# Queries doubled by transfers within SBUF, fox scores in two matmuls

## The chip, the cores and the metric

The kernel runs on one core of a Trainium2 chip, as one program. The metric is the device time of that core in microseconds (us), median of several executions. The engines are TensorE (PE in the profile), VectorE (DVE), ScalarE (ACT), GpSimd (POOL) and SyncE (SP, which here issues transfers only).

## The reference

Two transformer blocks follow each other on 512 positions of width 1024, in fp32. The first (latent attention beside a state-space scan, about 345 us) is not touched. The second has two layers, each with an attention mixer and an MLP of width 4096. The mixer has 8 "nsa" heads, each with a compressed, a selected and a window branch, and 8 "fox" heads, all of 64 dimensions. A fox head is causal attention in which running sums of log forget gates are added to the scores:

```python
log_f = jax.nn.log_sigmoid(f_logits.astype(jnp.float32) + f_bias.astype(jnp.float32))
cum = jnp.cumsum(log_f, axis=1).transpose(0, 2, 1)
for i in range(s // Q_BLOCK):
    q0, q1 = i * Q_BLOCK, (i + 1) * Q_BLOCK
    logits = (jnp.einsum('bhqd,bhkd->bhqk', q[:, :, q0:q1], k[:, :, :q1]).astype(jnp.float32) * scale
              + cum[:, :, q0:q1, None] - cum[:, :, None, :q1])
    mask = jnp.arange(q1)[None, :] <= jnp.arange(q0, q1)[:, None]
    p = _masked_softmax(logits, mask)
    outs.append(jnp.einsum('bhqk,bhkd->bhqd', p.astype(v.dtype), v[:, :, :q1]))
```

The term of the query, `cum[..., q0:q1, None]`, is the same along a row and falls out of the softmax; only that of the key is computed. With 512 positions all eight blocks of 64 keys are selected for every query, so that the selected and the window branch of an nsa head are each causal attention over all 512 keys, with rotated queries and keys of their own.

## The kernel before

TensorE gets fp32 accuracy from fp32r operands by splitting a number into a high part `hi` and the rest `lo`. A projection takes three matmuls a tile (hi by hi, hi by lo, lo by hi; lines 174 to 176). For scores the 64 dimensions leave half of the 128 contraction rows free, and the kernel fills them. `stacked` puts the keys' hi into one half and their lo into the other, for both heads of a pair (tiles `ka`, `kb`). `doubled` puts the queries' hi into both halves (`qh1`, `qh2`), and their lo into both halves (`ql1`, `ql2`). Then a score tile is two matmuls: the queries' hi over hi and lo of the keys (line 911), and the queries' lo over the same (line 914). A fox head has a third between them (line 913): a one-hot weight, `ohr`, picks the head's running sums out of `cumr`, which holds hi and lo of the sums of all heads on rows of their own. `attend` runs this for four blocks of 128 queries, over 512, 384, 256 and 128 keys, each followed by a VectorE instruction that adds the mask and takes the row's extreme (line 915), ScalarE's exponential (918), POOL's scaling (927), transposes on TensorE (940), a split of the transposed weights by ScalarE and VectorE (`pt`, lines 143 and 144) and the products with the values (949, 950).

`doubled` starts from a projected pair of heads: head 1 in partitions 0 to 63, head 2 in 64 to 127. ScalarE copies the hi part of all (871) and two halves into the other place (873, 875), VectorE copies the hi half that stays (874), POOL subtracts for lo in one instruction of 128 partitions (`lo`, 864), and VectorE copies three halves of it (876 to 878). It runs 8 times a layer: for four pairs of nsa queries, behind the rope, and for four pairs of fox queries.

The rope swaps rows of a pair by four small transfers that ScalarE's queue issues into a `swap` tile (1065); VectorE multiplies it (1066), POOL multiplies the source (1067), VectorE adds (1068). There are NSW = 2 such tiles, used in turn, first by the two tiles of nsa keys (`kf`) and then by the query pairs.

The order of the heads is n0 f0 n1 f1 n2 f2 n3 f3 (pairs). The 12 projections of query and key pairs run as fillers between the steps of the heads, so that a pair is projected shortly before it is attended; their weights are loaded one job ahead or more. The order of instructions on each engine is fixed when the program is built, by a scheduler that simulates a timeline; tiles come from pools with a given number of slots (`S`, `Q`, `PT`, `K`), and a tile that reuses a slot waits for the slot's last reader. SP issues all weight loads in its order.

Of the kernel before, what the change touches and what calls it, by code (L numbers as in the profile page):

```python
# [9 lines left out]
F32 = mybir.dt.float32  # L10
# [17 lines left out]
SL0 = 3  # L28
NSW = 2
UP = (3,)  # L30
# [6 lines left out]
BANKS2 = {"g": (0, 6), "sc": (0, 3), "o": (3, 5), "mm": (5, 6), "tr": (6, 8)}  # L37
SLOTS2 = {"S": 12, "PT": 6, "K": 4, "Q": 8, "c": 2, "ch": 1, "tb": 3, "e8": 2, "w": 4}

# [24 lines left out]
class Net:  # L64
# [782 lines left out]
    def setup2(self):  # L847
        c = lambda n, sh: self.const(n, sh, pool=self.spool)
        nc = self.nc
        self.mask = c("mask", [128, 512])  # L850

        self.swaps = [self.spool.tile([128, 512], F32, name=f"swap{i}") for i in range(NSW)]
        for t in self.swaps:
            nc.gpsimd.memset(t, 0.0)
        self.swap = itertools.cycle(self.swaps)
        self.cmask = c("cmask", [128, 4, 31])
        cv = c("cvalid", [128, 5])
        self.cvalid, self.sgn = cv[:, 0:4], cv[:, 4:5]
        oh = c("onehot", [128, 8])
        self.oh = self.spool.tile([128, 8], F32R, name="ohr")  # L860
        nc.vector.tensor_copy(self.oh, oh)

    def lo(self, out, src, hi):
        self.nc.gpsimd.tensor_tensor(out, src, hi.bitcast(F32), OP.subtract)

    def doubled(self, src, tag):

        nc = self.nc
        h1, h2, l1, l2 = (self.act(F32R, name=n, tag=tag) for n in ("qh1", "qh2", "ql1", "ql2"))
        lw, up = slice(0, 64), slice(64, 128)  # L870
        nc.scalar.copy(h1, src)
        self.lo(l1, src, h1)
        nc.scalar.copy(h2[lw], src[up])
        nc.vector.tensor_copy(h2[up], h1[up].bitcast(F32))
        nc.scalar.copy(h1[up], src[lw])
        nc.vector.tensor_copy(l2[up], l1[up].bitcast(F32))
        nc.vector.tensor_copy(l2[lw], l1[up].bitcast(F32))
        nc.vector.tensor_copy(l1[up], l1[lw].bitcast(F32))
        return (h1, l1), (h2, l2)

    def stacked(self, src, tag):
# [9 lines left out]

    def attend(self, q, k, rgate, v, o, first, last, cum=None):

# [9 lines left out]
        for group in ((3,), (2,), (0, 1)):  # L903
            bank = self.ps("sc")
            c = 0
            for i in group:
# [3 lines left out]
                c += w  # L910
                mm(p, q[0][:, qs], k[:, :w], start=True, stop=False)  # L911
                if cum is not None:
                    mm(p, cum[0], cum[1][:, :w], start=False, stop=False)
                self.pe = mm(p, q[1][:, qs], k[:, :w], start=False, stop=True)  # L914
                nc.vector.tensor_tensor_reduce(out=sreg[i], in0=p, in1=self.mask[:, 512 - w:512],  # L915
# [79 lines left out]
    def layer(self, l, normed, x_dram, out=None):  # L995
# [96 lines left out]
        def project(j):  # L1092
# [14 lines left out]
            if i == 0:  # L1107
                yield
                nsat[m] = self.doubled(rope(r, None), "Q")
            elif i == 1:  # L1110
                foxt["q", m] = self.doubled(r, "Q")
            else:
                foxt["k", m] = self.stacked(r, "PT")

# [35 lines left out]
        def fox_head(m, n, o):  # L1150
            k, q = foxt["k", m], foxt["q", m]
            h = m * 2 + n
            yield from self.attend(q[n], k[n], None, lambda j: vf[h // 4][:, j, h % 4],
                                   lambda: bank(o, "o"), True, True,
                                   cum=(self.oh[:, h:h + 1].to_broadcast([128, 128]), cr))
            mix(("f", m), n, o[0])

        def nsa_head(hp, n, b, o):
            gi = hp // 2
            yield from self.attend(nsat[hp][n], kk[b][gi], gv[:, 1 + b, 2 * hp + n],  # L1160
                                   lambda j: vs[:, j, b * 2 + gi], lambda: bank(o, "o"), b == 0, False)
# [362 lines left out]
```

## Time and profile before

| | |
|---|---|
| median of 3 runs | 1678.02 us (1675.13 to 1678.33) |
| profiled execution | 1678.21 us, span 1676.4 us |
| granted clock, mean | 0.985 |
| busy TensorE / VectorE / ScalarE / POOL | 1593.9 / 981.1 / 804.9 / 381.6 us |
| attention of layer 0 | about 420 to 610 us |
| attention of layer 1 | about 1088 to 1275 us |

In a row of the trace, the tiles stand as written<-read, without buffer numbers, then partitions x elements and type; a bracket gives the idle time of the engine just before the instruction and what ended it. "ACTq" and "SPq" are the queues of transfers that ScalarE and SP issue. The duration of a matmul includes the filling of the pipeline, so that what a row of matmuls costs is read from start to start.

### The profile page before, as it was taken

Reading aid. Unit: us, or ns where it says so; the run is one execution under the profiler, and the core shown is the slowest. Engines: PE = TensorE matmul, PEld = TensorE weight load, DVE = VectorE, ACT = ScalarE, POOL = GpSimd, SP = SyncE. Lnnn points to the kernel's source line nnn. Section 1 sums busy time; section 2 is a strip of 40 time slices with the busy share of each in tenths; the row PEclk is TensorE's granted clock in tenths of the full one; section 3 lists DMA queues with packets and bytes.
Section 4 is the critical chain, followed back from the end, with each engine's and each line's share of the span. In section 5 each row is a group of like instructions: output and inputs, shape, how many; then the busy total and the mean of one; then the engine's idle time right before and its main releaser. Section 6 shows DMA issues by size and latency. Waiting matters only on the chain.

```text
span 1676.4 us, 22515 instructions
## 1 busy us (share of the span) xinstructions
PE 1593.9 (95%) x8240; PEld 1344.6 (80%) x8240; DVE 981.1 (59%) x1927; ACT 804.9 (48%) x1564; POOL 381.6 (23%) x476
## 2 busy tenths in 40 slices
PE   7996799999999999999999999999989999999998
PEld 5885687787877788888888888788878888888886
DVE  7978767754798965323333355589885532333334
ACT  6734476533677844333242434367774433323242
POOL 2000112313345612101010131335471210101012
PEclk9998999999999999999999999999989999999999
DMA  5211452544210241333333333501123133333322
GB/s 169 76 56 38 128 146 75 184 119 150 66 40 26 79 149 51 101 100 101 101 101 90 98 110 114 193 15 40 40 76 126 51 101 101 101 100 101 100 90 87
DMA packets 66287, 159.04 MB, mean 95 GB/s; under 512 B 13440, under 2 KB 22144, under 8 KB 66176
## 3 DMA queue, kind: packets, MB, share of 16 engines
q1 hardware_dynamic: 65408, 156.81, 29.8%
q8 instruction: 65, 1.06, 0.3%
q10 hardware_dynamic: 768, 0.79, 0.2%
q14 instruction: 46, 0.38, 0.1%
HBM read 145.80 MB, written 10.98 MB: 94 GB/s over the span
## 4 chain that ended last, share of the span: by engine, by line
PE 71%; DVE 8%; ACT 3%; issue 2%; POOL 1%; DMA 1%; ACTq 0%; DVEq 0%; POOLq 0%
PE mm L174 20%; PE mm L176 20%; PE mm L175 20%; PE ptr L940 2%; PE cps L980 2%; DVE sc L915 2%; DVE pt L144 1%; PE sc L911 1%; PE oacc L950 1%; PE sc L914 1%; PE oacc L949 1%; ACT ysq L206 1%; DMA swap<-raw 1%; ACT sc L918 1%; POOL rs_r L201 1%
## 5 line engine op out<-in xcount | busy, mean ns | idle before, releaser
L144 DVE TENSOR_TENSOR wlo<-wst,whi 128x1024 fp32r<-128x1024 f32 (+3 forms) x209 | 253.7, 1218 | 250.5 <-ACT whi L143 246.7
L174 PE MATMUL mm<-xT,whi 128*128 128x512 f32 (+1 forms) x896 | 338.9, 381 | 4.2 <-ACT kf L1080 2.8
L143 ACT CAST whi<-wst 128x1024 fp32r<-128x1024 f32 (+3 forms) x209 | 215.4, 1034 | 256.4 <-PE mm L176 122.5
L175 PE MATMUL mm<-xT,whi 128*128 128x512 f32 (+1 forms) x896 | 336.9, 377 | 0.0
L176 PE MATMUL mm<-xT,wlo 128*128 128x512 f32 (+1 forms) x896 | 327.6, 378 | 1.0 <-DVE wlo L144 1.0
L174 PEld LDWEIGHTS mm<-xT,whi 128*128 128x128 f32 x896 | 169.4, 190 | 33.1 <-ACT kf L1080 3.6
L176 PE MATMUL mm<-whi,hl 128*128 128x512 f32 x512 | 195.9, 389 | 0.0
L175 PE MATMUL mm<-wlo,hh 128*128 128x512 f32 x512 | 195.9, 389 | 0.0
L176 PEld LDWEIGHTS mm<-xT,wlo 128*128 128x128 f32 x896 | 170.3, 190 | 31.7 <-DVE wlo L144 1.6
L175 PEld LDWEIGHTS mm<-xT,whi 128*128 128x128 f32 x896 | 170.4, 191 | 27.6
L1364 POOL TENSOR_TENSOR relu<-relu 128x512 f32<-128x512 f32 x64 | 67.0, 1047 | 539.8 <-ACT relu L1363 539.8
L174 PE MATMUL mm<-whi,hh 128*128 128x512 f32 x512 | 188.2, 389 | 0.0
L918 ACT ACTIVATE sc<-sc,mn 128x512 f32<-128x512 f32 x192 | 107.3, 561 | 33.9 <-DVE mn L915 30.6
L144 DVE TENSOR_TENSOR hl<-relu,hh 128x512 fp32r<-128x512 f32 x64 | 51.8, 810 | 119.7 <-ACT hh L143 117.5
L144 DVE TENSOR_TENSOR pt<-ptr,pt 128x256 fp32r<-128x256 f32 (+1 forms) x160 | 95.9, 606 | 31.5 <-ACT pt L143 30.0
L176 PEld LDWEIGHTS mm<-whi,hl 128*128 128x128 f32 x512 | 96.1, 188 | 20.1
L175 PEld LDWEIGHTS mm<-wlo,hh 128*128 128x128 f32 x512 | 96.1, 188 | 19.9
L174 PEld LDWEIGHTS mm<-whi,hh 128*128 128x128 f32 x512 | 96.1, 188 | 19.8
L1363 ACT ACTIVATE relu<-mm 128x512 f32<-128x512 f32 x64 | 38.4, 599 | 148.7 <-PE mm L176 148.7
L143 ACT CAST pt<-ptr 128x256 fp32r<-128x256 f32 (+1 forms) x160 | 81.7, 517 | 50.4 <-PE ptr L940 40.4
L915 DVE CUSTOM_DVE_ANT_0 sc<-sc,c_mask 128x512 f32<-128x512 f32 x192 | 87.9, 484 | 25.6 <-PE sc L914 23.7
L927 POOL TENSOR_SCALAR sc<-sc,smx,gt 128x512 f32<-128x512 f32 (+3 forms) x128 | 80.8, 641 | 93.5 <-DVE smx L922 65.8
(400 smaller groups left out, 2972.3 us busy)
## 6 DMA issues: line engine op xcount, KB each, us to landing
wst<-in_w_up_t SPq DMA_DIRECT2D x64, 512.0 KB
wst<-in_w_down_t SPq DMA_DIRECT2D x64, 512.0 KB
wst<-in_w_in_m SPq DMA_DIRECT2D x24, 512.0 KB
wst<-in_w_in_a SPq DMA_DIRECT2D x16, 512.0 KB
x<-x SPq DMA_DIRECT2D x32, 256.0 KB
w<-in_cw SPq DMA_DIRECT2D x32, 256.0 KB
wst<-in_w_out_t SPq DMA_DIRECT2D x16, 512.0 KB
wst<-in_w_in SPq DMA_DIRECT2D x8, 512.0 KB
```

The source lines that it names most:

```text
L143: self.nc.scalar.copy(hi, src)
L144: self.nc.vector.tensor_tensor(lo, src, hi.bitcast(F32), OP.subtract)
L174: mm(ps, lh, rh, start=first, stop=False)
L175: mm(ps, lh, rl, start=False, stop=False)
L176: mm(ps, ll, rh, start=False, stop=last)
L915: nc.vector.tensor_tensor_reduce(out=sreg[i], in0=p, in1=self.mask[:, 512 - w:512], scale=1.0, scalar=3e38, op0=OP.add, op1=OP.min, accum_ ...
L918: self.mark = nc.scalar.activation(sreg[i], sreg[i], AF.Exp, bias=mn[:, i:i + 1], scale=-1.0, accum_out=sm[:, i:i + 1])
L927: nc.gpsimd.tensor_scalar(sreg[i], sreg[i], sm[:, i:i + 1], rgate[:, i:i + 1], OP.mult, OP.mult)
L940: self.pe = nc.tensor.transpose(p[:, c:c + 128], sreg[i][:, j * 128:(j + 1) * 128], self.ident)
L980: nc.tensor.matmul(p[:, :62], st[:, j], bk[:, jj].rearrange("p g n -> p (g n)"), start=jj == 0, stop=jj == 15)
L1363: nc.scalar.activation(a, p, AF.Relu)
L1364: nc.gpsimd.tensor_tensor(a, a, a, OP.mult)
```

## The change

`doubled` copies hi by ScalarE to each head's own half only, and a transfer within SBUF, issued by SP (`move`), fills the other half; POOL subtracts lo for each head apart, on 64 partitions, and two more transfers double it. `fox_queries` does this for hi only; lo goes to the head's half of a tile `fq`, whose other half is zero but for two rows of ones. `fox_keys` makes a tile `fk` for each head by transfers: a copy of the stacked keys, in which the two rows that face the ones are overwritten by hi and lo of the head's running sums. So a fox score has two matmuls: the queries' hi over `ka`, and `fq` over `fk`. In the half that faces the zeros `fk` keeps the lo of the keys, which adds nothing; the product of lo by lo is left out in fox heads.

```diff
@@ -26,7 +26,7 @@
 R0, C0, LEAD, RATE0, RATE, AHEAD = 0, 1, 1, 1.3, 0.4, 5
 HEAD0 = (0, 3, 6, 9)
 SL0 = 3
-NSW = 2
+NSW = 1
 UP = (3,)
 ORD1 = "x0 g0 p0 x1 w0 w1 w2 w3 x2 x3"
 P0, RATE3 = 40, 2
@@ -35,7 +35,7 @@
 W = 12
 BANKS1 = {"g": (0, 6), "sc": (0, 2), "o": (2, 4), "mm": (4, 6), "tr": (6, 8)}
 BANKS2 = {"g": (0, 6), "sc": (0, 3), "o": (3, 5), "mm": (5, 6), "tr": (6, 8)}
-SLOTS2 = {"S": 12, "PT": 6, "K": 4, "Q": 8, "c": 2, "ch": 1, "tb": 3, "e8": 2, "w": 4}
+SLOTS2 = {"S": 11, "PT": 6, "K": 4, "Q": 6, "F": 4, "c": 2, "ch": 1, "tb": 3, "e8": 2, "w": 4}
 
 
 def rounds(items, heads=()):
@@ -856,27 +856,57 @@
         self.cmask = c("cmask", [128, 4, 31])
         cv = c("cvalid", [128, 5])
         self.cvalid, self.sgn = cv[:, 0:4], cv[:, 4:5]
-        oh = c("onehot", [128, 8])
-        self.oh = self.spool.tile([128, 8], F32R, name="ohr")
-        nc.vector.tensor_copy(self.oh, oh)
 
     def lo(self, out, src, hi):
         self.nc.gpsimd.tensor_tensor(out, src, hi.bitcast(F32), OP.subtract)
+
+    def move(self, out, src):
+        self.nc.sync.dma_start(out.bitcast(F32), src.bitcast(F32))
 
     def doubled(self, src, tag):
 
         nc = self.nc
         h1, h2, l1, l2 = (self.act(F32R, name=n, tag=tag) for n in ("qh1", "qh2", "ql1", "ql2"))
         lw, up = slice(0, 64), slice(64, 128)
-        nc.scalar.copy(h1, src)
-        self.lo(l1, src, h1)
-        nc.scalar.copy(h2[lw], src[up])
-        nc.vector.tensor_copy(h2[up], h1[up].bitcast(F32))
-        nc.scalar.copy(h1[up], src[lw])
-        nc.vector.tensor_copy(l2[up], l1[up].bitcast(F32))
-        nc.vector.tensor_copy(l2[lw], l1[up].bitcast(F32))
-        nc.vector.tensor_copy(l1[up], l1[lw].bitcast(F32))
+        nc.scalar.copy(h1[lw], src[lw])
+        nc.scalar.copy(h2[up], src[up])
+        self.move(h1[up], h1[lw])
+        self.move(h2[lw], h2[up])
+        self.lo(l1[lw], src[lw], h1[lw])
+        self.lo(l2[up], src[up], h2[up])
+        self.move(l1[up], l1[lw])
+        self.move(l2[lw], l2[up])
         return (h1, l1), (h2, l2)
+
+    def fox_queries(self, src):
+
+        nc = self.nc
+        h1, h2 = (self.act(F32R, name=n, tag="Q") for n in ("qh1", "qh2"))
+        lw, up = slice(0, 64), slice(64, 128)
+        nc.scalar.copy(h1[lw], src[lw])
+        nc.scalar.copy(h2[up], src[up])
+        self.move(h1[up], h1[lw])
+        self.move(h2[lw], h2[up])
+        q2 = [self.act(F32R, name="fq", tag="F") for _ in range(2)]
+        for i, (own, h) in enumerate(((lw, h1), (up, h2))):
+            r = 64 * (1 - i)
+            nc.gpsimd.memset(q2[i][r:r + 64].bitcast(F32), 0.0)
+            nc.gpsimd.memset(q2[i][r:r + 2].bitcast(F32), 1.0)
+            self.lo(q2[i][own], src[own], h[own])
+        return (h1, q2[0]), (h2, q2[1])
+
+    def fox_keys(self, src, cr, h):
+
+
+        nc = self.nc
+        a, b = self.stacked(src, "PT")
+        k2 = [self.act(F32R, name="fk", tag="F") for _ in range(2)]
+        for n in range(2):
+            self.move(k2[n], (a, b)[n])
+            for i in range(2):
+                r = 64 * (1 - n) + i
+                self.move(k2[n][r:r + 1], cr[32 * i + h + n:32 * i + h + n + 1])
+        return (a, k2[0]), (b, k2[1])
 
     def stacked(self, src, tag):
 
@@ -889,7 +919,7 @@
         self.lo(b[lw], src[up], b[up])
         return a, b
 
-    def attend(self, q, k, rgate, v, o, first, last, cum=None):
+    def attend(self, q, k, rgate, v, o, first, last):
 
 
 
@@ -908,10 +938,8 @@
                 qs = slice(i * 128, (i + 1) * 128)
                 p = bank[:, c:c + w]
                 c += w
-                mm(p, q[0][:, qs], k[:, :w], start=True, stop=False)
-                if cum is not None:
-                    mm(p, cum[0], cum[1][:, :w], start=False, stop=False)
-                self.pe = mm(p, q[1][:, qs], k[:, :w], start=False, stop=True)
+                mm(p, q[0][:, qs], k[0][:, :w], start=True, stop=False)
+                self.pe = mm(p, q[1][:, qs], k[1][:, :w], start=False, stop=True)
                 nc.vector.tensor_tensor_reduce(out=sreg[i], in0=p, in1=self.mask[:, 512 - w:512],
                                                scale=1.0, scalar=3e38, op0=OP.add, op1=OP.min,
                                                accum_out=mn[:, i:i + 1])
@@ -1108,9 +1136,9 @@
                 yield
                 nsat[m] = self.doubled(rope(r, None), "Q")
             elif i == 1:
-                foxt["q", m] = self.doubled(r, "Q")
+                foxt["q", m] = self.fox_queries(r)
             else:
-                foxt["k", m] = self.stacked(r, "PT")
+                foxt["k", m] = self.fox_keys(r, cr, 2 * m)
 
         def ensure(i, m):
             while m not in nsat if i == 0 else ("qk"[i - 1], m) not in foxt:
@@ -1151,13 +1179,12 @@
             k, q = foxt["k", m], foxt["q", m]
             h = m * 2 + n
             yield from self.attend(q[n], k[n], None, lambda j: vf[h // 4][:, j, h % 4],
-                                   lambda: bank(o, "o"), True, True,
-                                   cum=(self.oh[:, h:h + 1].to_broadcast([128, 128]), cr))
+                                   lambda: bank(o, "o"), True, True)
             mix(("f", m), n, o[0])
 
         def nsa_head(hp, n, b, o):
             gi = hp // 2
-            yield from self.attend(nsat[hp][n], kk[b][gi], gv[:, 1 + b, 2 * hp + n],
+            yield from self.attend(nsat[hp][n], (kk[b][gi],) * 2, gv[:, 1 + b, 2 * hp + n],
                                    lambda j: vs[:, j, b * 2 + gi], lambda: bank(o, "o"), b == 0, False)
             if b == 1:
                 mm(o[0], vc[:, gi, n].rearrange("p i d -> p (i d)"), cht[hp], start=False, stop=True)
```

On TensorE, the scores of the first fox pair in layer 0, before:

```order
L911 MATMUL sc_4429<-ka_3940,qh1_4071 128x512
L913 MATMUL sc_4429<-cumr_3603,ohr_3294 128x512
L914 MATMUL sc_4429<-ka_3940,ql1_4073 128x512
L911 MATMUL sc_4437<-ka_3940,qh1_4071 128x384
L913 MATMUL sc_4437<-cumr_3603,ohr_3294 128x384
L914 MATMUL sc_4437<-ka_3940,ql1_4073 128x384
L911 MATMUL sc_4367<-ka_3824,qh2_3839 128x256
L914 MATMUL sc_4367<-ka_3824,ql2_3841 128x256
```

and after:

```order
L941 MATMUL sc_4433<-ka_3934,qh1_4073 128x512
L942 MATMUL sc_4433<-fk_3940,fq_4079 128x512
L941 MATMUL sc_4440<-ka_3934,qh1_4073 128x384
L942 MATMUL sc_4440<-fk_3940,fq_4079 128x384
L941 MATMUL sc_4371<-ka_3818,qh2_3833 128x256
L942 MATMUL sc_4371<-ka_3818,ql2_3835 128x256
```

The 128-row `fk` and `fq` stand where `ka` and `ql1` stood, and the matmul of `cumr` by `ohr` is gone from each triple.

On ScalarE, the start of layer 0's attention, where the two key tiles `kf` are rotated and the first query pair `raw` follows, before:

```order
L1065 DMA swap0_3284<-kf_3734 8x512 x4
L1080 ACTIVATE kf_3761<-mm_3736 128x512
L143 CAST whi_3912<-wst_3910 128x1024
L1065 DMA swap1_3285<-kf_3761 8x512 x4
L143 CAST whi_4040<-wst_4038 128x1024
L1106 ACTIVATE raw_3800<-mm_3769 128x512
L886 CAST ka_3810<-kf_3734 64x512
L887 CAST kb_3811<-kf_3734 64x512
L1065 DMA swap0_3284<-raw_3800 8x512 x2
L886 CAST ka_3824<-kf_3761 64x512
```

and after:

```order
L1093 DMA swap0_3284<-kf_3728 8x512 x4
L1108 ACTIVATE kf_3755<-mm_3730 128x512
L143 CAST whi_3906<-wst_3904 128x1024
L143 CAST whi_4042<-wst_4040 128x1024
L1134 ACTIVATE raw_3794<-mm_3763 128x512
L916 CAST ka_3804<-kf_3728 64x512
L917 CAST kb_3805<-kf_3728 64x512
L1093 DMA swap0_3284<-kf_3755 8x512 x4
L1134 ACTIVATE raw_3932<-mm_3856 128x512
L916 CAST ka_3818<-kf_3755 64x512
L917 CAST kb_3819<-kf_3755 64x512
L1093 DMA swap0_3284<-raw_3794 8x512 x4
```

The second key tile's swap, which stood fourth, stands behind the casts of the first tile's stacked keys, and the first queries' swap behind the casts of the second's.

On SP at the same place, before (`w1` are weights of the compressed branch):

```order
L977 DMA w1_3976<-in_cw1 128x512
L971 DMA b1_9660<-in_cb1 128x2
L977 DMA w1_3995<-in_cw1 128x512
L977 DMA w1_4011<-in_cw1 128x512
L1174 DMA w2k_9765<-in_cw2 128x256
L1176 DMA b2k_9767<-in_cb2k 128x1
```

and after:

```order
L1005 DMA w1_3978<-in_cw1 128x512
L999 DMA b1_9662<-in_cb1 128x2
L864 DMA fk_3940<-ka_3934 128x512
L864 DMA qh1_3832<-qh1_3832 64x512
L864 DMA qh2_3833<-qh2_3833 64x512
L864 DMA fk_3940<-cumr_3597 1x16x32
L864 DMA ql1_3834<-ql1_3834 64x512
L864 DMA fk_3940<-cumr_3597 1x16x32
L864 DMA ql2_3835<-ql2_3835 64x512
L864 DMA fk_3941<-kb_3935 128x512
L1201 DMA w2k_9775<-in_cw2 128x256
L1005 DMA w1_3997<-in_cw1 128x512
```

Eight moves for the first nsa pair and the first fox keys stand between the weight loads; SP issues in this order.

On VectorE, the last fox pair of layer 0, before (`mn` is the mask reduction's result):

```order
L915 ISA sc_5997,mn_6000<-sc_6002,c_mask_3282 128x512
L915 ISA mn_6000 128x1
L915 ISA sc_5998,mn_6000<-sc_6012,c_mask_3282 128x384
L915 ISA mn_6000 128x1
L874 CAST qh2_5865<-qh1_5864 64x512
L876 CAST ql2_5867<-ql1_5866 64x512
L877 CAST ql2_5867<-ql1_5866 64x512
L144 TENSOR_TENSOR pt_5879<-ptr_5882,pt_5879 128x512
L878 CAST ql1_5866<-ql1_5866 64x512
L144 TENSOR_TENSOR pt_5880<-ptr_5889,pt_5880 128x512
```

and after:

```order
L943 ISA sc_5919,mn_5920<-sc_5942,c_mask_3282 128x256
L943 ISA mn_5920 128x1
L943 ISA sc_6007,mn_6010<-sc_6012,c_mask_3282 128x512
L943 ISA mn_6010 128x1
L943 ISA sc_6008,mn_6010<-sc_6022,c_mask_3282 128x384
L943 ISA mn_6010 128x1
L144 TENSOR_TENSOR pt_5889<-ptr_5892,pt_5889 128x512
L950 RECIPROCAL smx_5921<-smx_5921 128x2
L144 TENSOR_TENSOR pt_5890<-ptr_5899,pt_5890 128x512
```

The four copies between the reductions and `pt` are gone.

On POOL at the same place, before:

```order
L927 TENSOR_SCALAR sc_5907<-sc_5907,smx_5911,gt_3439 128x512
L864 TENSOR_TENSOR ql1_5866<-raw_5862,qh1_5864 128x512
L927 TENSOR_SCALAR sc_5908<-sc_5908,smx_5911,gt_3439 128x384
L864 TENSOR_TENSOR wo_5953<-wst_5954,wo_5953 128x512 x2
L927 TENSOR_SCALAR sc_5908<-sc_5908,smx_5911,gt_3439 128x128
L927 TENSOR_SCALAR sc_5909<-sc_5909,smx_5911,gt_3439 128x256
L927 TENSOR_SCALAR sc_5997<-sc_5997,smx_6001,gt_3439 128x512
```

and after:

```order
L955 TENSOR_SCALAR sc_5917<-sc_5917,smx_5921,gt_3433 128x512
L861 TENSOR_TENSOR fq_5878<-raw_5870,qh1_5872 64x512
L955 TENSOR_SCALAR sc_5918<-sc_5918,smx_5921,gt_3433 128x384
L861 TENSOR_TENSOR fq_5879<-raw_5870,qh2_5873 64x512
L861 TENSOR_TENSOR wo_5963<-wst_5964,wo_5963 128x512 x2
L955 TENSOR_SCALAR sc_5918<-sc_5918,smx_5921,gt_3433 128x128
L955 TENSOR_SCALAR sc_5919<-sc_5919,smx_5921,gt_3433 128x256
L955 TENSOR_SCALAR sc_6007<-sc_6007,smx_6011,gt_3433 128x512
```

One subtraction of 128 partitions is now two of 64, into `fq`, with a scaling of scores between them, and those of `wo` follow.

## Rows read from the trace of the kernel before

**Rows 1.** The page: the length of the span.
```profile
span 1676.4 us, 22515 instructions
```

**Rows 2.** Stretches: start:end, length, busy of PE, PEld, DVE, ACT, POOL, clock, DMA.
```profile
420.00:610.00 190.00, 178.62 (x1046) 152.04 (x1045) 157.79 (x461) 137.94 (x348) 94.21 (x127) 0.99 0.20 63
...
1088.00:1275.00 187.00, 175.40 (x1030) 151.71 (x1028) 155.29 (x458) 134.83 (x344) 93.52 (x125) 0.97 0.13 42
```

**Rows 3.** Chain of waits in 420:610: shares by line, one piece (start, us).
```profile
by line: DVE sc L915 9.0%; DVE pt L144 7.4%; PE ptr L940 6.6%; PE mm L176 5.8%; PE mm L174 5.7%; PE mm L175 5.6%; DMA swap<-raw 4.9%; issue 4.0%; DVE mix L1148 3.3%; PE sc L911 3.2%; PE sc L914 3.2%; ACT pt L143 3.0%; PE oacc L950 2.8%; PE 
...
451.48 3.62 DMA swap<-raw
```

**Rows 4.** Chain of waits in 1088:1275: shares by line, one piece.
```profile
by line: PE ptr L940 10.6%; PE mm L174 9.9%; PE mm L176 9.8%; PE mm L175 9.6%; PE sc L911 6.3%; PE sc L914 5.7%; PE oacc L950 5.2%; PE oacc L949 5.0%; DVE sc L915 4.7%; PE cps L980 3.3%; ACT sc L918 3.3%; DVE pt L144 2.7%; issue 2.5%; PE sc
...
1119.07 1.98 DMA swap<-raw
```

**Rows 5.** TensorE in 450:457 (start, us, line, tiles): one fox head.
```profile
450.88 0.40 PE L913 MATMUL sc<-cumr,ohr 128*128 128x512 f32 x1
451.12 0.39 PE L914 MATMUL sc<-ka,ql 128*128 128x512 f32 x1
...
456.63 0.27 PE L913 MATMUL sc<-cumr,ohr 128*128 128x128 f32 x1
456.74 0.28 PE L914 MATMUL sc<-ka,ql 128*128 128x128 f32 x1
```

**Rows 6.** Groups by line and shape (busy us, mean ns | idle before, releaser).
```profile
L874 DVE CAST qh<-qh 64x512 fp32r<-64x512 f32 x16 | 11.8, 736 | 1.8 <-ACT qh L871 1.4
...
L876 DVE CAST ql<-ql 64x512 fp32r<-64x512 f32 x16 | 9.1, 571 | 2.7 <-POOL ql L864 2.4
...
L877 DVE CAST ql<-ql 64x512 fp32r<-64x512 f32 x16 | 8.7, 544 | 0.2
...
L878 DVE CAST ql<-ql 64x512 fp32r<-64x512 f32 x16 | 7.0, 439 | 0.5
...
L864 POOL TENSOR_TENSOR kb<-raw,kb 64x512 fp32r<-64x512 f32 x8 | 11.2, 1406 | 0.6
...
L1196 POOL MEMSET hv<- 128x512 f32 x2 | 1.1, 525 | 1.5 <-PE cps L980 1.5
```

**Rows 7.** One by one in 583:587, last fox pair of layer 0.
```profile
583.92 1.40 DVE L877 CAST ql<-ql 64x512 fp32r<-64x512 f32 x1
...
586.10 0.44 PE L940 MATMUL ptr<-c_ident,sc 128*128 128x128 f32 x2 [2.04 <-DVE pt L144]
```

**Rows 8.** TensorE at 1249.9, last fox pair of layer 1.
```profile
1249.90 0.58 PE L911 MATMUL sc<-kb,qh 128*128 128x256 f32 x1 [1.86 <-DVE mn L915]
```

**Rows 9.** Stretches: two at a lowered clock.
```profile
586.00:590.00 4.00, 3.58 (x13) 2.91 (x14) 2.32 (x11) 1.47 (x5) 2.37 (x4) 0.66 0.53 142
...
1250.00:1256.00 6.00, 5.45 (x15) 4.22 (x16) 2.73 (x10) 1.79 (x7) 4.24 (x7) 0.50 0.29 90
```

**Rows 10.** One by one in 392:422, start of attention in layer 0.
```profile
396.79 2.64 ACTq L1065 DMA_DIRECT2D swap<-kf  x4
...
402.64 1.29 DVE L1068 TENSOR_TENSOR kf<-swap,r 128x512 f32<-128x512 f32 x2
...
412.78 1.41 DVE L1066 TENSOR_TENSOR swap<-swap,ld_ropeS 128x512 f32<-128x512 f32 x1 [8.85 <-DMA swap<-raw]
...
415.90 0.62 ACT L871 CAST qh<-r 128x512 fp32r<-128x512 f32 x1 [2.96 <-DVE r L1068]
...
419.04 0.42 DVE L878 CAST ql<-ql 64x512 fp32r<-64x512 f32 x1
...
419.57 0.56 PE L911 MATMUL sc<-ka,qh 128*128 128x512 f32 x2
...
421.08 0.69 DVE L915 CUSTOM_DVE_ANT_0 sc<-sc,c_mask 128x512 f32<-128x512 f32 x1
```

**Rows 11.** Stretch before the first scores of layer 0.
```profile
404.00:420.00 16.00, 16.00 (x109) 14.63 (x108) 5.14 (x8) 6.95 (x12) 10.51 (x8) 1.00 0.52 184
```

## Prediction

> **What bounds the kernel now.** The profiled execution took 1678.21 us, of which the span is 1676.4 [rows 1] and 1.8 lies around it; the median of the runs shown is 1678.02, so sums made against the one hold for the other. I read the stretches by engine first. The change touches only the attention of the second block, two stretches of 190 and 187 us. In them TensorE is busy 178.6 and 175.4 us, about 94%, and VectorE 157.8 and 155.3, about 83% [rows 2]. Neither is free: what is taken from TensorE counts in part, what is taken from VectorE counts where TensorE waits for it.
>
> So the second view is the chain of waits, which says which engine the end hangs on. In layer 0 the printed lines give TensorE 6.6+5.8+5.7+5.6+3.2+3.2+2.8 = 32.9% and VectorE 9.0+7.4+3.3 = 19.7%; in layer 1 TensorE has 10.6+9.9+9.8+9.6+6.3+5.7+5.2+5.0+3.3 = 65.4% and VectorE 7.4% [rows 3, 4]. The cut lists make these lower bounds. The reader is to see that the two layers, with the same work, have different limits: layer 0 goes back and forth between engines, layer 1 is mostly TensorE.
>
> The third view is the idle time of TensorE by its releaser. The largest hole of layer 0's attention behind the doubling is at the last fox pair: 2.04 us, released by VectorE's `pt` of line 144, which stood behind the doubling copies 876 and 877 [rows 7]. Layer 1 has 1.86 us at the same pair, released by VectorE's mask reduction [rows 8]. Behind both the granted clock is lowered: 0.66 in a stretch of 4 us, and 0.50, the 1.2 GHz level, in one of 6 us [rows 9].
>
> **The change part by part.**
>
> The matmul of the running sums goes. Its pitch, from its start to that of the next matmul, is 0.24 us for 512 columns and 0.11 for 128 [rows 5]; the two widths between, in proportion, take 0.18 and 0.12. That is 0.65 us a head and 16 heads: 10.4 us of TensorE, 5.2 a layer. The second matmul of the pair is as wide as the third was, with other operands, and costs the same. What of it reaches the end I take by TensorE's share of the chain: 5.2 x 0.33 + 5.2 x 0.65 = 5.1 us. Bounds: 0 (others set the pace) to 10.4.
>
> The four VectorE copies a call go: 11.8 + 9.1 + 8.7 + 7.0 = 36.6 us in 16 calls [rows 6], 18.3 a layer. A microsecond of VectorE is worth its share of the chain over its busy share: 0.197/0.83 = 0.24 in layer 0, 0.074/0.83 = 0.09 in layer 1, which gives 4.4 + 1.6 = 6.0. Some 2 of these lie in the last pairs and are counted next, so 4 remain. Bounds: 0 to 36.6.
>
> At the last fox pair VectorE no longer has the copies in its order between two mask reductions and `pt`. The hole and the slow clock behind it are 2.04 + 1.86 of idling and 4 x 0.34 + 6 x 0.50 = 4.4 of lost clock, 8.3 us. I take three quarters, 6.2, because the moved data can be late in its turn: POOL now has two subtractions of 1.4 us there for one, and `wo`'s still behind them. Bounds: 0 to 8.3.
>
> One copy of ScalarE a call goes as well, the other two become 64 partitions wide; the engine is busy 138 of 190 us [rows 2], and I count nothing: its exponentials wait for VectorE's reductions, and if that cover is gone the gain is at most the 8 copies of 0.62 us [rows 10] a layer.
>
> POOL gains 8 subtractions a layer at 1.41 us, since 64 partitions cost there what 128 do, and 8 memsets at 0.53 at most beside 8 small ones: 11.3 + 4.2 + 0 to 4.2, some 17 us on 94 [rows 2, 6]. It stays under 60% busy, so I count nothing for the load itself. What it costs in contention is bounded by one row: copy 877 took 1.40 us beside POOL's `wo` [rows 7], against 0.42 of its sibling 878 [rows 10]. So a VectorE tensor operation beside a POOL one may be stretched by 0.98; 16 added POOL operations a layer, with 0.24 and 0.09 of that on the path, would cost 5 us at most. This lies inside the bound of the VectorE term, which loses copies that were stretched that way.
>
> The Trainium skill ("SBUF — State Buffer", Who interferes with whom) gives a rule that speaks against the subtractions: a VectorE operation with two SBUF inputs, or a fast copy, and a GpSimd one that reads SBUF hold a lock against each other, and the second waits for the whole of the first, while TensorE, ScalarE and DMA do not wait. The rows just named agree in kind: 1.40 for 0.42. By the rule each of the 8 added subtractions a layer could stop VectorE for its 1.41 us; with the shares above that is 8 x 1.41 x (0.24 + 0.09) = 3.7 us, and the sum below would be -5.6 instead of -9.3.
>
> The moves are 48 DMAs a layer: 16 of 128 KB for the nsa queries, 8 for the fox queries, 8 of 256 KB and 16 of single rows for the fox keys. Nothing else in these stretches moves SBUF to SBUF but the rope swap; its wait stands in the chain with 1.98 us in layer 1 and 3.62 in layer 0 [rows 3, 4], where the DMA engines are busier (0.20 for 0.13 [rows 2]). I take 2 to 3.6 for a move. They replace copies that ended 0.1 us before the first score wanted them (878 ends at 419.46, the score starts at 419.57 [rows 10]), so at a pair that is that tight the added latency is felt; where a pair is made well ahead it is hidden by the other heads. SP waits in order for each move's source, so a weight load behind it starts later; those loads lead by several projections, and I count nothing for them. If that cover is gone, a projection starts late by about a subtraction plus a move, 3 to 5 us.
>
> The start of attention has a price of its own. With one swap tile for two (NSW), the swap of the second key tile, issued at 396.79 before, waits for the first one's addition (first of the two that start at 402.64) and stands behind two casts on ScalarE: 402.64 + 0.65 + 2 x 0.62 = 404.5. It issues for 2.64 us and lands some 2 later, at 409.2, then a multiplication and an addition of 0.65 to 0.7; the first query's swap follows at 410.6 at the earliest and lands, issue and latency again, at 415.2 to 417, where before it was multiplied at 412.78 [rows 10]. So rope is late by 2.4 to 4.2 us. From rope to the first score it was 3.7 us (415.90 to 419.57); now cast 0.62, subtraction 1.4 and move 2 to 3.6 make 4 to 5.6. The first mask reduction, at 421.08, would be late by 3 to 6. TensorE is 16.00 of 16 us busy ahead of it [rows 11], and now has the rest of the third projection, 12 matmuls of 0.24, before its first score; that shields 2.9 us of the delay, but VectorE and ScalarE begin later. I take 3 us a layer, 6 in all; bounds 0 to 16.
>
> Sum: -5.1 - 4.0 - 6.2 + 6.0 = -9.3. From 1678.2 that is 1668.9 us, say 1669.
>
> **The rivals.**
>
> A, VectorE is the pace. If the chain's sharing understates it, because every stall of TensorE in layer 0 goes back to VectorE, half of the 36.6 us counts: -5.1 - 18 - 6.2 + 6 = -23, 1655. For it: 83% busy and 157.8 us in layer 0 [rows 2]. Against: in layer 1 VectorE has 7.4% of the chain [rows 4].
>
> B, the gain is hidden. TensorE's holes move to the next wait, the pairs wait for moves in place of copies, and the start costs its 6: -5.1 + 6 = about +1, within what a measurement tells (0.2%, 3.4 us: 1674.8 to 1681.6). For it: no engine alone is the bound in layer 0 [rows 3].
>
> C, the moves are late. The place is the pairs that are made just ahead of their use: beside the first of each layer, which is in the start, I take three a layer (the third and fourth nsa pair and the last fox pair). If a move takes over 4 us, behind the queue on SP and beside weight loads, each such pair stalls TensorE by about 3 us, the swap's 3.62 less what a copy took, and the clock falls behind it as in [rows 9]. Then the last-pair gain is gone: -5.1 - 4 + 6 + 6 x 3 = +15, 1693. For it: DMA share 0.52 at the start [rows 11] and 0.53 at the last pair [rows 9]. Against: DMA share 0.20 and 0.13 over the stretches [rows 2].
>
> That the change doesn't do what it says is no rival: both orders show the matmuls and copies gone.
>
> **How the numbers follow.** The forecast has 0.45 (1661 to 1674.5); A 0.16, B 0.16, C 0.23. A and the forecast are faster, 0.61; B is the same, with a hundredth or two to the other side, 0.15; C is slower, 0.24. The range goes from 1654, half of A, to 1685, short of C's middle; the forecast's own is 1661 to 1675.
>
> **What would show it.** Right: no matmul of the sums; score starts 0.65 us a head closer; no VectorE copy in front of the last `pt`, and holes there under 1 us with the clock at full; first mask reduction 3 us later than 421.08, TensorE still busy ahead of it. Wrong: score matmuls with idle time released by moves, on several pairs (C); a stretch of layer 0 shorter by over 10 us while layer 1's is not (A); the same holes with other releasers (B).

## The result and the profile after

The changed kernel takes 1687.23 us (median of 7 runs, 1680.91 to 1691.26) against 1676.62 for the kernel before in the same comparison. The ratio is 1.0056, with a 95% interval of 1.0039 to 1.0073: slower by some 9.4 us, where 9.3 us faster was forecast. The profiled execution took 1687.87 us, its span 8.6 us more than that of [rows 1].

The page of the changed kernel has the span, then busy time of each engine:

```profile
span 1685.0 us, 22595 instructions
...
PE 1598.6 (95%) x8176; PEld 1344.5 (80%) x8176; DVE 952.7 (57%) x1862; ACT 792.5 (47%) x1548; POOL 409.7 (24%) x523
```

VectorE is busy 28 us less than before, and POOL 28 more. TensorE has 64 matmuls less and is busy 5 us longer. Matmuls that became fewer and took longer point to the clock, so the next view is the two attention stages of each kernel, cut into start and rest. Columns: start:end, length, busy time of PE, PEld, DVE, ACT, POOL with counts, granted clock, DMA share, GB/s. First before:

```profile
400.00:460.00 60.00, 57.29 (x366) 50.13 (x364) 38.16 (x110) 35.03 (x86) 27.83 (x32) 1.00 0.32 105
460.00:620.00 160.00, 150.63 (x853) 127.28 (x851) 134.98 (x372) 116.35 (x283) 77.66 (x103) 0.99 0.22 71
1060.00:1130.00 70.00, 66.95 (x409) 57.99 (x407) 46.95 (x127) 39.47 (x92) 29.37 (x34) 1.00 0.32 102
1130.00:1300.00 170.00, 159.70 (x889) 137.07 (x889) 136.88 (x374) 117.45 (x293) 78.78 (x103) 0.97 0.21 70
```

Then after:

```profile
400.00:460.00 60.00, 54.36 (x309) 46.82 (x308) 27.71 (x80) 26.86 (x64) 25.43 (x30) 0.91 0.39 118
460.00:620.00 160.00, 149.56 (x848) 125.45 (x847) 125.78 (x365) 116.08 (x294) 94.70 (x130) 0.99 0.31 93
1060.00:1130.00 70.00, 63.34 (x328) 53.73 (x326) 31.64 (x85) 27.17 (x63) 26.98 (x31) 0.88 0.36 112
1130.00:1300.00 170.00, 160.56 (x919) 137.32 (x918) 137.48 (x381) 122.82 (x303) 94.36 (x128) 0.99 0.31 94
```

Length less PE's busy time is idle; length times (1 - clock) is what the clock took. At the two starts (first and third row) idling goes from 2.7 + 3.1 to 5.6 + 6.7 us, 6.5 more, and the clock takes 60 x 0.09 + 70 x 0.12 = 13.8 us where it took nothing. In the rest of the stages idling is about the same (19.7 and 19.9), and the clock takes 1.6 + 1.7 for 1.6 + 5.1, 3.4 less. With 10.4 us of matmuls gone this makes 6.5 + 13.8 + 0.2 - 3.4 - 10.4 = +6.7 of the 8.6 us. Over the whole span the same count closes: idling goes from 1676.4 - 1593.9 = 82.5 to 86.4 us, and the clock, 0.985 in the mean before and 0.976 now, takes 40.4 us for 25.1, so that 3.9 + 15.3 - 10.4 = +8.8.

At the start of layer 0, one by one, the rows that answer to [rows 10]:

```profile
403.55 0.63 ACTq L1093 DMA_DIRECT2D swap<-kf  x1
...
407.06 1.53 ACTq L1093 DMA_DIRECT2D swap<-kf  x2
...
411.61 0.69 DVE L1094 TENSOR_TENSOR swap<-swap,ld_ropeS 128x512 f32<-128x512 f32 x1 [8.19 <-DMA swap<-kf]
...
417.39 1.31 DVE L1094 TENSOR_TENSOR swap<-swap,ld_ropeS 128x512 f32<-128x512 f32 x1 [4.28 <-DMA swap<-raw]
...
418.80 1.58 DVE L1096 TENSOR_TENSOR r<-swap,r 128x512 f32<-128x512 f32 x1
...
420.31 0.27 DVE L1015 TENSOR_TENSOR cu<-cx 128x124 f32<-128x124 f32 x1
...
420.42 0.62 ACT L871 CAST qh<-r 64x512 fp32r<-64x512 f32 x1 [2.65 <-DVE r L1096]
...
421.20 1.29 DVE L1019 TENSOR_SCALAR cx<-cx 128x124 f32<-128x124 f32 x1
...
421.70 1.28 ACT L1018 ACT_TABLE_LOAD   x1
...
423.00 0.31 ACT L1018 ACTIVATE cu<-cu 128x124 f32<-128x124 f32 x1
...
423.34 0.57 DVE L1020 SCALAR_TENSOR_TENSOR cx<-cu,cx 128x124 f32<-128x124 f32 x1 [0.85 <-ACT cu L1018]
...
423.96 0.66 PE L1207 MATMUL c2ps<-cx,w2k 128*128 128x62 f32 x4 [0.59 <-DVE cx L1020]
...
424.43 0.71 PE L941 MATMUL sc<-ka,qh 128*128 128x512 f32 x3
...
425.70 0.70 PE L942 MATMUL sc<-ka,ql 128*128 128x512 f32 x3 [0.56 <-DMA ql<-ql]
...
426.21 0.69 DVE L943 CUSTOM_DVE_ANT_0 sc<-sc,c_mask 128x512 f32<-128x512 f32 x1 [2.30 <-PE sc L942]
...
427.05 1.21 PE L1246 MATMUL cs<-zk,raw 128*128 128x62 f32 x8 [0.65 <-DVE mn L943]
```

The second key tile's swap is issued at 403.55, 6.8 us later than before; the first queries' swap is multiplied, as soon as it has landed, at 417.39 for 412.78; the first mask reduction is at 426.21 for 421.08, 5.1 late. In VectorE's order the steps of the compressed branch (`cu`, `cx`, lines 1015 to 1020) stand behind the late rope, and so do ScalarE's casts of the queries (line 871 and its like). VectorE has its part of `cu` ready at 421.2, but ScalarE's step on it (line 1018) stands behind two casts and a table load of 1.28 us and starts at 423.00; line 1020, the last step of `cx`, waits 0.85 us for that. TensorE's `c2ps`, which needs `cx`, now stands ahead of the first scores, where before the first score stood ahead of it. So TensorE waits three times within 4 us (0.59, 0.56, and 0.65 ahead of `cs` at 427); the second of these waits is for a move. In layer 1 the chain is the same, and the first of the waits is longer:

```profile
1098.37 0.66 PE L1207 MATMUL c2ps<-cx,w2k 128*128 128x62 f32 x4 [2.18 <-DVE cx L1020]
```

Behind both the clock falls to its 1.2 GHz level for 8 to 10 us:

```profile
428.00:436.00 8.00, 7.85 (x35) 7.27 (x34) 3.65 (x13) 4.28 (x12) 5.39 (x8) 0.50 0.75 235
1102.00:1112.00 10.00, 10.00 (x38) 9.13 (x38) 5.11 (x21) 4.34 (x12) 6.12 (x9) 0.50 0.66 197
```

At the last fox pairs the places of [rows 7, 8] have waits of 0.41 us, for a move, and 0.92:

```profile
593.03 0.47 PE L941 MATMUL sc<-ka,qh 128*128 128x512 f32 x1 [0.41 <-DMA qh<-qh]
```

```profile
1261.59 0.38 PE L941 MATMUL sc<-kb,qh 128*128 128x256 f32 x1 [0.92 <-DVE mn L943]
```

Other holes stand near them: 1.17 and 1.10 us a little later, beside the last pair's scores, released by softmax sums, and in layer 1 one of 1.95 us in the fox pair before.

```profile
601.53 0.63 PE L968 MATMUL ptr<-c_ident,sc 128*128 128x128 f32 x4 [1.17 <-DVE smx L950]
```

```profile
1239.61 0.44 PE L968 MATMUL ptr<-c_ident,sc 128*128 128x128 f32 x2 [1.95 <-DVE pt L144]
...
1274.39 0.63 PE L968 MATMUL ptr<-c_ident,sc 128*128 128x128 f32 x4 [1.10 <-DVE smx L950]
```

Around the last pairs the clock is full in layer 0 and little lowered in layer 1, where [rows 9] had 0.66 and 0.50. Before:

```profile
575.00:610.00 35.00, 32.63 (x186) 28.12 (x185) 25.83 (x73) 22.79 (x59) 17.53 (x25) 0.95 0.45 134
1225.00:1275.00 50.00, 45.81 (x251) 38.72 (x250) 36.06 (x105) 33.94 (x85) 27.54 (x35) 0.93 0.18 56
```

After:

```profile
575.00:610.00 35.00, 31.99 (x186) 26.95 (x185) 23.94 (x83) 25.21 (x68) 26.35 (x37) 1.00 0.43 128
1235.00:1285.00 50.00, 43.98 (x240) 36.80 (x239) 36.80 (x104) 33.91 (x85) 32.12 (x43) 0.97 0.37 105
```

So the clock came back there, but TensorE's idling did not shrink: 2.4 and 4.2 us before, 3.0 and 6.0 now.

### The profile page after: what moved, and what is told of

Same layout as the page of the kernel before. It is cut to its first block, busy times and chain, and to the rows that moved or that the text cites. A ratio compares the mean times of both kernels' runs of the same rounds, so it can differ in the third digit from the quotient of the medians.

```text
span 1685.0 us, 22595 instructions
## 1 busy us (share of the span) xinstructions
PE 1598.6 (95%) x8176; PEld 1344.5 (80%) x8176; DVE 952.7 (57%) x1862; ACT 792.5 (47%) x1548; POOL 409.7 (24%) x523
## 5 line engine op out<-in xcount | busy, mean ns | idle before, releaser
L175 PEld LDWEIGHTS mm<-wlo,hh 128*128 128x128 f32 x512 | 96.1, 188 | 19.9
```

Source lines behind the costliest of these rows:

```text
L175: mm(ps, lh, rl, start=False, stop=False)
```

## Experiments

Theory S says the one swap tile costs the time, by the late start of each layer. Its rival, theory M, is the prediction's rival C: pairs wait for moves. All ratios are against the kernel before on the same chip, with the 95% interval.

**One swap tile alone, in the kernel before.**

```diff
-NSW = 2
+NSW = 1
```

> The kernel before with one swap tile for two (NSW = 1) and nothing else. Theory S (the one swap tile is what costs: the second key tile's swap waits for the first one's rope, and the whole start of attention and a slow clock behind it follow): 6 to 10 us slower than before, the first mask reduction of layer 0 at 424 to 426 us for 421.1, and a stretch of lowered clock within 20 us behind it. Theory M (the moves are late at the pairs): within 2 us of before.

1691.11 us, ratio 1.0096 [1.0070, 1.0122]: 16 us slower. TensorE waits at the same three places of layer 0's start as in the changed kernel, without any move in the program:

```profile
424.73 0.66 PE L1180 MATMUL c2ps<-cx,w2k 128*128 128x62 f32 x4 [1.28 <-DVE cx L992]
...
426.17 1.18 PE L914 MATMUL sc<-ka,ql 128*128 128x512 f32 x3 [0.26 <-DVE ql L878]
427.81 1.94 PE L1219 MATMUL cs<-zk,raw 128*128 128x62 f32 x8 [0.46 <-DVE mn L915]
```

```profile
426.00:438.00 12.00, 11.38 (x46) 10.66 (x47) 7.04 (x29) 7.06 (x21) 5.12 (x8) 0.51 0.52 167
1108.00:1122.00 14.00, 14.00 (x68) 13.01 (x67) 7.05 (x25) 5.56 (x16) 5.25 (x9) 0.60 0.00 1
```

(The profiled execution is the slowest of its five, 1698.81 us.) Theory S holds in kind, at a price above its range of 6 to 10 and with the first mask reduction at 426.96, behind its 424 to 426; theory M's, within 2 us, fails.

**Two swap tiles in the changed kernel.**

```diff
-NSW = 1
+NSW = 2
...
-SLOTS2 = {"S": 11, "PT": 6, "K": 4, "Q": 6, "F": 4, "c": 2, "ch": 1, "tb": 3, "e8": 2, "w": 4}
+SLOTS2 = {"S": 10, "PT": 6, "K": 4, "Q": 6, "F": 4, "c": 2, "ch": 1, "tb": 3, "e8": 2, "w": 4}
```

> The changed kernel with two swap tiles again; one slot of S is given up to make room (11 to 10). Theory S: 8 to 15 us faster than the changed kernel, 1670 to 1678, first mask reduction of layer 0 at 421 to 423. Theory M: within 3 us of the changed kernel, 1684 to 1690, first mask reduction still at 425 or later.

1663.99 us, ratio 0.9948 [0.9923, 0.9972]. Against the changed kernel that is 0.9948/1.0056 = 0.9893, 18 us less, which is more than theory S's 8 to 15; theory M's, within 3 us, fails. Of its 12 runs two are at 1679 and 1682 and the profiled one is of these. In it the first mask reduction is at 423.80, and the clock fell at the start of layer 1 (0.88 over 1060:1130, which is 8.4 us), and not in layer 0. Behind a wait for a weight load that ten moves stand ahead of in SP's order it was at 0.50 for some 16 us:

```profile
1091.05 1.10 PE L1008 MATMUL cps<-bk,w 128*128 128x62 f32 x8 [1.16 <-DMA w<-in_cw]
```

```profile
1095.00:1108.00 13.00, 13.00 (x54) 12.23 (x53) 4.71 (x20) 3.16 (x10) 3.20 (x4) 0.50 0.12 36
```

```profile
1086.27 1.85 SPq L864 DMA_DIRECT2D fk<-cumr  x3
1088.18 5.55 SPq L1005 DMA_DIRECT2D w<-in_cw  x7
```

The profiled execution has a mean clock of 0.979, the 12 together 0.987, so the clock differs between executions of one and the same program; where it stayed up in the others no trace shows.

**Moves in the kernel before.** `doubled` as in the changed kernel for nsa and fox queries; two swap tiles, three matmuls, the old slots.

```diff
...
-        nc.vector.tensor_copy(l2[up], l1[up].bitcast(F32))
-        nc.vector.tensor_copy(l2[lw], l1[up].bitcast(F32))
-        nc.vector.tensor_copy(l1[up], l1[lw].bitcast(F32))
+        nc.scalar.copy(h1[lw], src[lw])
+        nc.scalar.copy(h2[up], src[up])
+        self.move(h1[up], h1[lw])
+        self.move(h2[lw], h2[up])
...
+        self.move(l1[up], l1[lw])
+        self.move(l2[lw], l2[up])
```

> The kernel before with the doubling by moves for nsa and fox queries alike, with two swap tiles, the slots of before and the fox scores in three matmuls. Theory S: within 4 us of before, to the faster side, since the copies are gone from VectorE. Theory M: 6 us or more slower than before, with TensorE idle before scores that wait for moves.

1668.26 us, ratio 0.9953 [0.9935, 0.9970], 7.9 us faster, where theory S allowed 4. It has 32 moves a layer, four for each of the eight query pairs; of the changed kernel's 48, 24 are for queries. Theory M falls, as far as the queries go.

**The copies of before for the nsa queries, in the changed kernel.** `doubled` as in the kernel before, `fox_queries` as in the changed one:

```diff
...
-        self.move(l1[up], l1[lw])
-        self.move(l2[lw], l2[up])
...
+        nc.vector.tensor_copy(l2[up], l1[up].bitcast(F32))
+        nc.vector.tensor_copy(l2[lw], l1[up].bitcast(F32))
+        nc.vector.tensor_copy(l1[up], l1[lw].bitcast(F32))
```

> The changed kernel with the copies of before for the nsa queries only; the fox heads keep two matmuls, their moves, and one swap tile. Theory S: still 4 to 9 us slower than before, since the swap tile stays one. Theory M: 3 to 8 us faster than before, since the nsa pairs have no moves to wait for and the third matmul is gone.

1679.97 us, ratio 1.0024 [1.0007, 1.0041], 4 us slower than before. Theory S expected 4 to 9; it is at the edge. Against the changed kernel it is 5 us less, which is as much as the two intervals together leave open. Its start is earlier too: the queries' swap is multiplied at 414.16 and the first mask reduction is at 423.06, some 3 us before the changed kernel's, so the moves are not all that differs. The next two versions show no cost of the nsa pairs' moves once the start is early.

**Key tiles with swap tiles of their own.** In the changed kernel, the keys' rope takes two zeroed tiles of the fox slots, idle at that time; `a_fswap_dve` is the same with copies for the nsa queries.

```diff
-            t1, t2 = next(self.swap), self.act(name="r2", tag="S")
+            if dst is None:
+                t1 = next(self.swap)
+            else:
+                t1 = self.act(name="swk", tag="F")
+                nc.gpsimd.memset(t1, 0.0)
+            t2 = self.act(name="r2", tag="S")
```

> The changed kernel, where the two key tiles take a zeroed tile each out of the four slots of fox for their swap, so that only the queries use the one swap tile; all other slots as in the changed kernel. Theory S: the start is as early as with two swap tiles or earlier, 1660 to 1668, 12 to 20 us faster than the changed kernel. Theory M: 1680 or more.

> The same with the copies of before for the nsa queries, so only the fox heads' part of the change is left. If the moves serve the nsa queries well, it is 2 to 6 us slower than the version with moves; if they are late for the nsa pairs, 2 to 6 us faster; within 2 us if the copies of 8 calls are worth nothing.

Both have a median of 1665.03 us, ratios 0.9932 [0.9914, 0.9949] and 0.9928 [0.9910, 0.9947]: 11 to 12 us faster than before, and the fastest versions beside that with two swap tiles. Moves or copies for the nsa queries: no difference that can be told. The two starts of the version with moves:

```profile
400.00:460.00 60.00, 57.41 (x366) 50.51 (x366) 35.19 (x103) 35.14 (x85) 32.31 (x39) 1.00 0.43 131
...
1060.00:1130.00 70.00, 67.25 (x417) 58.23 (x415) 45.86 (x132) 43.20 (x105) 36.34 (x45) 1.00 0.40 125
```

Full clock in both. That the trick itself gives nothing was tried in the kernel before, with tiles of the query slots:

> The kernel before, where the two key tiles take a zeroed tile each out of the slots of the queries for their swap, so that the first queries' swap waits for neither. If an earlier start is worth something beside the two swap tiles of before: 2 to 5 us faster than before. If the start of before is hidden behind TensorE's projections, as its 16.00 of 16 busy us say: within 2 us of before. Either way the first mask reduction is expected at 418 to 421.

1674.54 us, ratio 1.0003 [0.9992, 1.0015]: nothing, though the first mask reduction came at 418.69, 2.4 us earlier than before. The gain of the two versions is the rest of the change, and a start earlier than that of before is worth nothing.

**The matmul of the sums alone.** In the kernel before, whose scores then lack the forget gates:

```diff
-                if cum is not None:
+                if False:
                     mm(p, cum[0], cum[1][:, :w], start=False, stop=False)
```

> The kernel before without the matmul of the running sums in the fox heads, so that its scores lack the forget gates; nothing else is changed. The prediction's term: 5.1 us faster than before (0 to 10.4). If VectorE and ScalarE set the pace there, 0 to 2; if TensorE does, 8 to 10.

1670.34 us, ratio 0.9963 [0.9948, 0.9978], 6.2 us faster; 5.1 was the term.

**The last fox pair alone.** In the kernel before, moves for that pair of each layer and copies for the others.

```diff
-                foxt["q", m] = self.doubled(r, "Q")
+                foxt["q", m] = (self.doubled_moves if m == 3 else self.doubled)(r, "Q")
```

> The kernel before, in which only the last fox pair of each layer is doubled by moves; the other seven calls a layer keep their copies, and two swap tiles and three matmuls stay. The prediction's term for this pair: 6.2 us faster than before (0 to 8.3), with TensorE's holes of 2.04 and 1.86 us and the lowered clock behind them gone. If the moves are late there in their turn: within 2 us of before, with the holes released by transfers.

1670.44 us, ratio 0.9969 [0.9954, 0.9983], 5.2 us faster; 6.2 was the term. In layer 0 TensorE idles 0.4 us in the 35 around that pair, at full clock:

```profile
575.00:610.00 35.00, 34.57 (x200) 29.61 (x199) 23.86 (x70) 23.73 (x61) 17.79 (x25) 1.00 0.60 181
```

In layer 1 a move takes the hole's place, which may be why the term is not reached (waits of TensorE in 1225:1275: engine, line, releaser, us in total, times, longest):

```profile
PE sc L929 <- DMA qh<-qh: 2.5, 1, 2.5
```

**How much of the start is the clock?** Theory K says the clock behind the holes is most of it, theory L that it is the lateness. 12 matmuls that nothing uses fill the hole ahead of `c2ps`, first in the changed kernel:

```diff
+            for _ in range(12):
+                mm(p, nsat[0][0][0][0:64, 0:128], nsat[0][0][0][0:64], start=True, stop=True)
             for m in range(2):
                 mm(p[:, :62], w2[:, m].rearrange("p a d -> p (a d)"), X[0][:, m], start=m == 0, stop=m == 1)
```

> The changed kernel with 12 matmuls more a layer (64 rows, 512 columns) that compute nothing that is used, ahead of the compressed branch's second matmul at the start of attention. They add 24 x 0.24 = 5.8 us of TensorE. Theory K (what one swap tile costs is mostly the clock that falls behind TensorE's holes at the start): the lowered stretch of some 10 us at 428 and at 1101 us is gone, its 5 to 6 us a layer come back, and the kernel is 3 to 8 us faster than the changed one in spite of the added work, 1679 to 1684. Theory L (it is the late start itself): 3 to 6 us slower than the changed one.

1688.06 us, ratio 1.0067 [1.0047, 1.0086], for 1.0056 of the changed kernel: 2 us slower, with some 4 us of doubt. Theory K's 3 to 8 us faster does not fit; theory L's 3 to 6 slower lies within the doubt. But the version does not part the two cleanly. The holes ahead of `cs` are filled, the clock stays up until 432, and then TensorE meets a long wait for weights, where the changed kernel waits 0.15 us at most:

```profile
434.27 1.97 PE L1008 MATMUL cps<-bk,w 128*128 128x62 f32 x8 [4.19 <-DMA w<-in_cw]
```

The order of SP moved with the filling. In the changed kernel `w2k` and a first `w` are issued ahead of the last two moves of `fk`; here they stand behind them:

```profile
426.21 0.59 SPq L864 DMA_DIRECT2D fk<-kb  x1
428.60 2.08 SPq L864 DMA_DIRECT2D fk<-cumr  x2
...
431.35 0.90 SPq L1005 DMA_DIRECT2D w<-in_cw  x2
```

The two rows of running sums, which SP issues after a wait of 1.8 us for the landing of the copy `fk<-kb` that they overwrite, hold the weights of the compressed branch until 431.35, and the clock falls behind this hole (0.61 over 432:445). The same filling where there are no moves, in the kernel before with one swap tile:

> The kernel before with one swap tile, and with 12 matmuls more a layer (64 rows, 512 columns, 5.8 us in all for both layers) that compute nothing that is used, ahead of the compressed branch's second matmul, where TensorE sits idle for 1.3 and 3.1 us in the version with one swap tile. There are no moves here that could hold a weight load up. Theory K (most of what one swap tile costs is the clock that falls behind that hole): the two lowered stretches of 12 us are gone and it is 5 to 10 us faster than the version with one swap tile in spite of the added work, 1681 to 1686. Theory L (it is the late start itself, the clock only takes what would be idle anyway): 2 to 6 us slower than that version, 1693 to 1697.

1691.70 us, ratio 1.0110 [1.0088, 1.0133]; the version without filling had 1.0096, so it is 2 us slower, with some 6 us of doubt. Theory K's 5 to 10 us faster fails, theory L's 2 to 6 slower is not excluded. In the profiled execution (1687.27 us) the clock is full in the first start and falls less in the second:

```profile
400.00:460.00 60.00, 55.60 (x346) 47.94 (x344) 33.72 (x101) 32.18 (x80) 24.40 (x29) 1.00 0.31 100
...
1060.00:1130.00 70.00, 65.91 (x373) 55.68 (x372) 39.02 (x103) 33.11 (x78) 24.45 (x28) 0.95 0.31 102
```

Over its 6 runs, though, the clock listed with each run is hardly higher than without the filling (mean 0.9813 for 0.9806). The order moves with the filling too: part of the third projection now stands behind the first scores. And the filling reads the late queries, so that in layer 1 it waits in its turn:

```profile
1092.47 4.22 PE L1180 MATMUL c2ps<-qh 64*128 64x512 f32 x12 [1.76 <-ACT qh L871]
```

So the filling does not keep the clock up reliably, and how much of the price would go with the clock alone stays open.

What the clock listed with each run does tell is the sum: (1 - mean clock) times mean time is 35.9 us in the 7 runs of the changed kernel and 23.8 in 25 runs of the kernel before, 12 more; with one swap tile alone 32.8, 9 of its 16 us; with the keys' own swap tiles 18.6.

## Why the prediction was wrong

The step that failed is the price of the start, in the prediction's words "I take 3 us a layer, 6 in all; bounds 0 to 16". The cause and the lateness were right: the second key tile's swap was put at 404.5 and was issued at 403.55; the landing of the queries' swap at 415.2 to 417, and it was 417.39; the first mask reduction late by 3 to 6, and it was 5.1. In between errors cancelled: the casts did not hold the key tile's swap up, but its four transfers took 5 us to issue instead of 2.64, and the queries' swap, put at 410.6 at the earliest, was issued from 413.22 and landed 4.2 us later, where 4.6 to 6.4 were reckoned. What it costs is 16 us (`b_nsw1`), in the changed kernel 18 to 21 (against `a_nsw2` and `a_fswap`). Two links were left out. First, other work stands behind the late rope in the orders of VectorE and ScalarE, the compressed branch's `cu` and `cx`, and TensorE's `c2ps` waits for it ahead of the scores; that 12 projection matmuls cover 2.9 us was counted, that nothing covers what follows them was not. Second, the clock falls behind these holes. The prediction read that pattern at the last pairs, gave it 4.4 us there [rows 9], and put it into rival C for pairs that wait for moves, but not into the price of the start.

The other terms, timed alone, stand. The matmul of the sums: 5.1 forecast, 6.2 measured. The last pairs: 6.2 forecast, 5.2 measured alone; in the changed kernel the clock is back there, but not the idling. The other copies: 4 forecast; `b_moves` less `b_f3` gives 7.9 - 5.2 = 2.7, and no gain by the nsa queries' part of them can be told between `a_fswap` and `a_fswap_dve`. They come to 14.1 for 15.3; together, in `a_fswap`, 11.4 are measured, so they don't quite add up, by 3 us that the intervals of the runs (about 3 us each) cover.

The contention of POOL and VectorE, weighed at 3.7 us by the rule of the Trainium skill ("SBUF — State Buffer", Who interferes with whom), was not seen as a loss of its own: `a_fswap` and `a_fswap_dve` differ by 4 subtractions, 16 copies and 16 moves a layer and take the same time, though what the copies gain may hide what the subtractions cost, and the intervals would not show 2 us. At the start of layer 0 `cx` of line 1019 took 1.29 us beside POOL's subtraction and 0.23 in the kernel before, so the kind of stretch is there, but it cost nothing at that place: line 1020 waited 0.85 us longer for ScalarE.

Rival A (VectorE sets the pace) falls: with 28 us of VectorE's work gone the rests of the stages, start apart, idle as long as before. Rival B has its mechanism in the rest of the stages, where holes went and others came, but not its size: with an early start the gain is 11 us. Rival C was the case on the slower side, and its sign came out, but its place is wrong: TensorE waited for moves in three scores of the whole program, 1.3 us together. That the moves in SP's order would cost nothing held in the changed kernel itself (0.15 us of waiting for those weights), but not in other orders: `a_warm` waits 4.19 us, where `b_nsw1_warm`, without moves, waits 1.03, and the profiled execution of `a_nsw2` lost 1.16 us that way and the clock behind them.

The chances gave 0.24 to slower, and the range ended at 1685. The upper bound of 16 us for the start stands without a working, and it was still too low: with it the sum is -15.3 + 16, or 1679 us. What was measured is 18 to 21 for the start, and 11 for 15.3 of gains.

## What to carry to other kernels

Taking a buffer away is an edit with a price of its own: follow its reuse through the orders of all engines to the first wait of the bound engine, and price the hole together with the clock behind it, here 6.5 us of idling and 13.8 of clock. Where the trace shows once that a hole of 1 to 2 us is followed by several us at a lowered clock (here 4 to 16), look for every place where the change can open another. A change with several parts is best timed with its parts apart: here the parts that were meant were worth 11 us, and a slot given up to make room for them cost 18 to 21.

## What the hardware showed that was not expected

In layer 0 the clock fell behind three short waits (0.59, 0.56, 0.65 us) and no longer one. One program (`a_nsw2`) took 1664 us in most executions, at a listed clock near 0.989, and 1679 and 1682 in two, at 0.979 and 0.975; that the difference arose at a start is seen in the one trace only, and for 8.4 us of it. POOL's memset of 2 partitions takes as long as that of 64:

```profile
L893 POOL MEMSET fq<- 64x512 f32 x16 | 8.3, 521 | 0.8
L894 POOL MEMSET fq<- 2x512 f32 x16 | 8.3, 518 | 0.8
```
